# mLSTM stabilisers on all partitions by a transfer through DRAM instead of by matmuls, and three heads in one written order on every engine

## The chip, the cores and the metric

The kernel runs on one core of a Trainium2 chip. The metric is the device time of one execution in microseconds (us). Engines are named as in the profile: PE (TensorE, matmuls) with PEld (its weight loads), DVE (VectorE), ACT (ScalarE), POOL (GpSimd) and SP (SyncE, which here only issues DMAs).

## What is computed

One layer of a hybrid backbone, all in float32: norm and modulation, one input projection, a bidirectional mLSTM (4 heads of width 128) beside a windowed attention, an output projection, and a gated channel mixer. There are 1024 latent tokens and 256 context tokens, width 1024. The change touches the mLSTM, which the reference computes for both directions, first over the context (for its final state) and then over the latent tokens:

```python
def mlstm_scan(q, k, v, log_i, log_f, init, return_h):
    k, v, li, lf = chunk(k), chunk(v), chunk(log_i), chunk(log_f)
    cum = jnp.cumsum(lf, axis=-1)
    cum_end = cum[..., -1]
    g = cum_end[..., None] - cum + li
    m_loc = jnp.max(g, axis=-1)
    w = jnp.exp(g - m_loc[..., None])
    c_loc = jnp.einsum('bhnsd,bhnse->bhnde', w[..., None] * k, v)
    ...
    def step(carry, inp):            # from chunk to chunk
        m_new = jnp.maximum(bt + m_st, m_l)
        a = jnp.exp(bt + m_st - m_new)
        s = jnp.exp(m_l - m_new)
        return (a * c_st + s * c_l, a * n_st + s * n_l, m_new), (c_st, n_st, m_st)
    ...
    a_log = cum + m0[..., None]
    d_log = cum[..., :, None] - cum[..., None, :] + li[..., None, :]
    d_log = jnp.where(order, d_log, -jnp.inf)
    m_t = jnp.maximum(a_log, jnp.max(d_log, axis=-1))        # the stabiliser
    dec = jnp.exp(d_log - m_t[..., None])
    inter = jnp.exp(a_log - m_t)
    s = jnp.einsum('bhntd,bhnsd->bhnts', q, k) * dec
    num = jnp.einsum('bhnts,bhnse->bhnte', s, v) + inter * jnp.einsum('bhntd,bhnde->bhnte', q, c0)
    den = jnp.sum(s, axis=-1) + inter * jnp.einsum('bhntd,bhnd->bhnt', q, n0)
    hid = num / jnp.maximum(jnp.abs(den), jnp.exp(-m_t))
```

The sum of both directions is normalised per head, and multiplied by a gain and the sigmoid of an output gate.

## The kernel before

The kernel works in chunks of 128 tokens: 2 of the context and 8 latent ones (`NC`, `NL`, together `NCH` = 10), and two directions `d`. Projections are made in a split of float32 into a high and a low part (`wh`, `wl`, `hl`), with three matmuls for each product.

**Gates.** `gate_chain` computes for all heads and chunks at once, with one token to a partition, the sums `cum`, the sources `a_` and the stabiliser `M_`, and from them the factors `gi`, `gfl`, `gw`, `gd`. For the decay matrix, the stabiliser is also needed along the free axis: the kernel keeps it in two parts, `mh` and `ml`.

**Heads.** A loop over four heads runs `mlstm(h)`, a generator of 30 steps, and between its steps pieces of another generator that fills PE: `dense(h + 1)`, the projections k, q, v and o of the next head (L537 and the three lines from L298 on), and in the last head `qgen()`, the projection q of the attention. At each step a budget grows by `RATE` us (`RATE3` in the last head; twice at the first step), and pieces are issued until it is used up. A piece names its own length, 0.64 or 1.28 us.

**Steps of `mlstm`.** Two steps with a transpose of a k chunk (`tr`, L601, into the psum tile `pn`; `kwb` and `kwf` are its copies weighted for the two directions), then nine of the backward state: the next transpose, a matmul into `pn` and the update of `cbk` (L631); then the two context chunks of the forward state (`step`, tile `cst`, L651 and L653), then per latent chunk one `first` and one `second`. `first` makes the scores (L664) and the exponent of the decay: three matmuls add, in one psum tile, the causal mask in units of 1e30 (`bigr`, L665) and the stabiliser on all partitions (a matrix of ones times `dm`, which POOL makes as identity times `mh` and `ml`, L660 and L661; L666 and L667). ACT takes the exponential of it into `ee`, DVE multiplies the scores in (L671). `second` multiplies with the states (`pj`, L680 and L681) and with `ee` (`pi`, L683), makes the next forward state, and on ACT and DVE the quotient `hid`.

**Beside that.** The normalisation and gating of a head (`finish`, L712 to L715) is issued in one block within the next head. The output gate's sigmoid is made in place in `ym`, with a tanh on ACT and two instructions on POOL (L641, L642). `ada_second` adds up parts of the adaLN product on DVE from loads of 256 KB (`w`, L731 to L735), eight to a sum, and PE then totals one (`pq`, L740); one whole sum is issued at three of the steps of a head. `load_split` loads weights `wr` and cuts them into `wh` (ACT) and `wl` (DVE, L152).

**Order.** Inside a head `tc.manual_schedule(engines={PE})` keeps the written order on PE alone; on the other engines a scheduler sets it. The psum tiles `pn`, `pe`, `pj`, `pi` and `pq` share a ring of four buffers (`pl`). All DMAs go through the queue of SP.

## Time and profile before

| | |
|---|---|
| time, median of 3 runs | 1331.45 us (1327.45 to 1332.98) |
| the profiled execution | 1331.05 us, its span 1329.1 us |
| busy over the span: PE, DVE, ACT, POOL | 1270.1 (96%), 1000.4 (75%), 610.1 (46%), 329.1 us (25%) |
| granted clock of TensorE, mean | 0.986 |
| the chain that ended last | PE 51%, DVE 8%, ACT 3%, DMA 2% |
| gate chain and projections of head 0 | 97 to 134 us |
| mLSTM of the four heads | 134 to about 400 us, 71 us for head 1 and for head 2 |

Busy time of an engine counts stretches in which it executes; the shares are averages over stages with different limits, so the heads have to be looked at by themselves.

### The profile page before, as it was taken

The numbers are of one execution on the slowest core, as the hardware profiler recorded it, in microseconds if no ns is written. First come the engines' busy times: TensorE is split into PE (matmuls) and PEld (weight loads), VectorE is DVE, ScalarE is ACT, GpSimd is POOL, SyncE is SP. The second block draws the span as 40 slices with busy tenths as digits, with TensorE's granted clock in tenths as the row PEclk, the third lists the DMA queues.
The fourth block names the chain that finished last, engine by engine and source line by source line (L and its number), as shares of the span: only waits on it lengthen the run. The fifth ranks groups of instructions, "written<-read, shape, count | busy, mean of one in ns | idle before, by whom it ended". The sixth has DMA issues, their size and how long they took to land.

```text
span 1329.1 us, 19745 instructions
## 1 busy us (share of the span) xinstructions
PE 1270.1 (96%) x7141; PEld 1082.2 (81%) x7141; DVE 1000.4 (75%) x1819; ACT 610.1 (46%) x1195; POOL 329.1 (25%) x388
## 2 busy tenths in 40 slices
PE   5889999999999899899989999999999999999997
PEld 4689899999989778788867788888888888788886
DVE  5644787866775788988688877777777776876887
ACT  6532244444555576676664333333333333444435
POOL 0440131313346223432330222222122223001000
PEclk9899899999989999999999999999999999999999
DMA  9430444340016422111431333222222325984663
GB/s 357 168 112 33 128 144 143 111 136 5 18 63 192 159 80 96 64 64 49 143 127 48 135 117 105 103 103 99 100 103 103 111 103 193 348 306 151 202 200 137
DMA packets 86017, 171.42 MB, mean 129 GB/s; under 512 B 12672, under 2 KB 25120, under 8 KB 85920
## 3 DMA queue, kind: packets, MB, share of 16 engines
q1 hardware_dynamic: 85632, 169.38, 37.5%
q8 instruction: 56, 0.92, 0.3%
...
q14 instruction: 41, 0.34, 0.1%
HBM read 131.84 MB, written 38.29 MB: 128 GB/s over the span
## 4 chain that ended last, share of the span: by engine, by line
PE 51%; DVE 8%; ACT 3%; DMA 2%; issue 1%; POOL 1%; SPq 0%; ACTq 0%; DVEq 0%; POOLq 0%
PE pd L1808 13%; PE pa L1300 8%; PE pc L1300 8%; PE pe L1300 4%; PE pb L1300 4%; PE pd L1300 4%; PE u L1070 2%; PE po L298 2%; PE po L300 1%; PE po L299 1%; DVE nm L1018 1%; PE pt L1047 1%; DVE hB L1190 1%; DMA ar<-act_s 1%; DVE wl L1190 1%
## 5 line engine op out<-in xcount | busy, mean ns | idle before, releaser
L1402 ACT CAST wh<-Rb 128x1024 fp32r<-128x1024 f32 (+1 forms) x66 | 59.5, 903 | 144.7 <-PE pd L1300 81.6
L1808 PE MATMUL pd<-dh,al 128*128 128x512 f32 x296 | 115.4, 390 | 1.2 <-DVE al L1174 1.2
L1808 PE MATMUL pd<-dh,ah 128*128 128x512 f32 x296 | 115.3, 389 | 0.4 <-ACT ah L1173 0.4
L1808 PE MATMUL pd<-dl,ah 128*128 128x512 f32 x296 | 115.3, 390 | 0.0
L1510 POOL TENSOR_TENSOR tt<-vt,tt 128x512 f32<-128x512 f32 x22 | 29.6, 1344 | 322.7 <-ACT tt L1504 322.7
L1300 PE MATMUL pc<-hB,wh 128*128 128x512 f32 x344 | 106.2, 390 | 1.1 <-DVE av L1379 1.1
L1300 PE MATMUL pa<-hB,wh 128*128 128x512 f32 x336 | 103.5, 389 | 0.0
L1190 DVE TENSOR_TENSOR wl<-Rb,wh 128x1024 fp32r<-128x1024 f32 (+1 forms) x66 | 68.8, 1044 | 39.3 <-ACT wh L1402 38.8
L537 PE MATMUL pp<-hl,wh 128*128 128x512 f32 x256 | 79.8, 403 | 0.0
L1300 PEld LDWEIGHTS pc<-hB,wh 128*128 128x128 f32 x344 | 64.5, 188 | 15.2 <-DVE av L1379 1.6
L298 PE MATMUL pv<-wh,hl 128*128 128x256 f32 x256 | 75.3, 294 | 0.0
L1300 PEld LDWEIGHTS pa<-hB,wh 128*128 128x128 f32 x336 | 63.0, 188 | 13.4 <-ACT sn L1474 0.3
L299 PE MATMUL pv<-wl,hl 128*128 128x256 f32 x256 | 72.8, 284 | 0.0
L300 PE MATMUL pv<-wh,hl 128*128 128x256 f32 x256 | 72.7, 284 | 0.0
L1300 PE MATMUL pc<-hB,wl 128*128 128x512 f32 x172 | 66.9, 389 | 0.0
L1808 PEld LDWEIGHTS pd<-dh,al 128*128 128x128 f32 x296 | 55.6, 188 | 13.4 <-DVE al L1174 1.9
L1808 PEld LDWEIGHTS pd<-dh,ah 128*128 128x128 f32 x296 | 55.6, 188 | 12.3 <-ACT ah L1173 0.8
L1300 PE MATMUL pa<-hB,wl 128*128 128x512 f32 x168 | 65.4, 389 | 0.0
L1808 PEld LDWEIGHTS pd<-dl,ah 128*128 128x128 f32 x296 | 55.6, 188 | 11.7 <-DVE dl L1174 0.3
L660 POOL TENSOR_SCALAR dm<-ident,mh 128x128 fp32r<-128x128 f32 x64 | 28.5, 446 | 131.7 <-PE pe L667 91.1
L298 PE MATMUL px<-wh,hl 128*128 128x256 f32 (+1 forms) x192 | 57.5, 299 | 2.8 <-ACT kr L321 2.8
L300 PE MATMUL px<-wh,hl 128*128 128x256 f32 (+1 forms) x192 | 55.2, 287 | 1.4 <-DVE hl L294 1.4
...
## 6 DMA issues: line engine op xcount, KB each, us to landing
...
br<-in_w_down_dram SPq DMA_DIRECT2D x25, 512.0 KB, 6.0
Ra<-in_w_up_dram SPq DMA_DIRECT2D x22, 512.0 KB, 3.6
Rb<-in_w_up_dram SPq DMA_DIRECT2D x22, 512.0 KB, 3.6
...
wr<-in_w_h_dram SPq DMA_DIRECT2D x16, 512.0 KB, 4.8
```

The lines of the kernel that those rows point to most:

```text
L298: T.matmul(ps, st_hi, mv_hi, start=first, stop=False)
L299: T.matmul(ps, st_hi, mv_lo, start=False, stop=False)
L300: T.matmul(ps, st_lo, mv_hi, start=False, stop=last)
L537: T.matmul(pp[:, 512 * n:512 * n + 512], wkq[sw][:, kt, cs], hl[n][part][:, kt, :], start=kt == 0 and sw + part == 0, stop=kt == KT - 1 an ...
L660: G.tensor_scalar(out=dm[:, d], in0=ident[:], scalar1=mhf[:, d, c, h:h + 1], scalar2=1.0, op0=ALU.mult, op1=ALU.mult)
L1018: V.tensor_reduce(out=self.nm[:, j:j + 1], in_=self.sv[j], axis=AX.X, op=ALU.max, negate=True)
L1070: T.matmul(self.u[:], vv[:, c, self.g], part[i][:, kk * 2 * P:(kk + 1) * 2 * P], start=kb + m == 0, stop=kb == last and m == 1)
L1190: sub = lambda e, o, x, y: e.tensor_tensor(out=o, in0=x, in1=y, op=ALU.subtract)
L1300: T.matmul(ps[:], wt[sw][:, j, ks], hB[part][:, blk, kt, :], start=first and kt == 0 and sw + part == 0, stop=last and kt == 3 and sw == 1 ...
L1402: S.copy(wt[0][:], src)
L1510: G.tensor_tensor(out=self.tt[:, h2_], in0=self.vt[:], in1=self.tt[:, h2_], op=ALU.mult)
L1808: T.matmul(ps[:], ac[sa][:, js], w[sw], start=first and n == 0, stop=last and n == 2, skip_group_check=not fresh)
```

## The change

**Stabiliser.** After the gate chain, two PE transposes turn `M_` into rows, DVE copies them into `rr`, and one DMA writes them to the new DRAM tile `m_d` (40 KB). At the start of each head, one DMA reads that head's 8 x 2 rows of 128 numbers onto all 128 partitions (`ee`, 1 MB, one buffer). DVE adds the mask to it chunk by chunk (`mask`, L619; `tri` is loaded anew with the mask in units of 1e30), ACT takes the exponentials in place (`decay`). The three matmuls, `dm`, `bigr`, `onesr`, `mh` and `ml` go.

**Order.** In heads 0 to 2 the written order now holds for all five engines; in head 3 for PE only, as before. What the scheduler spread before is now spread by hand: convolution and silu of the projections are cut into pieces (`todo`), of which one runs at each piece of the projection; `finish` gives one instruction to a step; `ada_second` gives one piece to a step, loads two ahead, and totals a sum four pieces after its end; raw weights are loaded steps ahead of their cuts.

**Moved.** `kwf`, the scaling of `hid` and the copy of `ym` go from DVE to ACT, the product of the output gate from POOL to DVE (one instruction), `step` from `second` to `first`. RATE goes from 1.4 to 1.5, QB (the latent chunk of v and o before which q is projected) from 2 to 3, TN (the step of the output gate) from 5 to 7.

The core of the diff:

```diff
-RATE = 1.4
+RATE = 1.5
-QB = 2
+QB = 3
-TN = 5
+TN = 7
...
+    m_d = kvp.tile([H * NCH, 2, P], F32, name="m_d")
...
     def gate_chain():
...
-        V.tensor_copy(fl(mh), fl(M_))
-        V.tensor_tensor(out=fl(ml), in0=fl(M_), in1=fl(mh).bitcast(F32), op=ALU.subtract)
...
+        pr = pl.tile([P, 512], F32, name="pr", tag="l")
+        for d in range(2):
+            T.transpose(pr[:40, d * P:d * P + P], M_[:, d].rearrange("p c h -> p (c h)"), ident[:])
+        V.tensor_copy(rr[:], pr[:40, 0:2 * P].rearrange("p (d t) -> p d t", d=2))
+        nc.sync.dma_start(m_d[:], rr[:])
+
+        nc.sync.dma_start(tri[:], I["cst"][:, 3:5])
+        yield
...
+    def conv_silu(dst, ps, w, cb):
+        return [lambda: S.activation(dst, ps[:, :w], AF.Identity, bias=spc("qkc", cb + 3), scale=spc("qkc", cb + 1)),
+                None,
+                lambda: V.scalar_tensor_tensor(out=dst[:, 1:w], in0=ps[:, 0:w - 1], scalar=spc("qkc", cb),
+                                               in1=dst[:, 1:w], op0=ALU.mult, op1=ALU.add),
+                lambda: V.scalar_tensor_tensor(out=dst[:, 0:w - 1], in0=ps[:, 1:w], scalar=spc("qkc", cb + 2),
+                                               in1=dst[:, 0:w - 1], op0=ALU.mult, op1=ALU.add),
+                None,
+                lambda: S.activation(ps[:, :w], dst, AF.Tanh),
+                None,
+                lambda: V.scalar_tensor_tensor(out=dst, in0=ps[:, :w], scalar=1.0, in1=dst, op0=ALU.add, op1=ALU.mult)]
...
+        def work(w):
+            f = todo.pop(0) if todo else None
+            if f:
+                f()
+            return w
...
-                yield 1.28
...
+                yield work(1.28)
+            todo.extend(conv_silu(kT[:, CTX:] if which == 0 else qT[:], pp, SEQ, cb))
...
-            marks.append(V.tensor_copy(ym[:, b, h * DH:(h + 1) * DH], pv[:, DH:2 * DH]).ins)
...
+            S.copy(ym[:, b, h * DH:(h + 1) * DH], pv[:, DH:2 * DH])
...
     def mlstm(h, kT, qT, va):
...
+        ee = tp.tile([P, NL, 2, P], F32, name="ee", tag="ee", bufs=1)
+        nc.sync.dma_start(ee[:], m_d[:].rearrange("(c h) d t -> h c d t", h=H)[h:h + 1, NC:].broadcast_to([P, NL, 2, P]))
...
-                V.tensor_scalar(out=kwf[:, c], in0=pn[:, 0:P], scalar1=g1(gw, 0, c), scalar2=None, op0=ALU.mult)
+                S.activation(kwf[:, c], pn[:, 0:P], AF.Copy, scale=g1(gw, 0, c))
             return pn, kwb
+
+        def mask(b):
+            V.tensor_tensor(out=ee[:, b], in0=ee[:, b], in1=tri[:], op=ALU.add)
+
+        def decay(b):
+            for d in range(2):
+                S.activation(ee[:, b, d], ee[:, b, d], AF.Exp, bias=g1(a_, d, NC + b), scale=-1.0)
...
-            if i == FN and fins:
-                with tc.issue_after(kins[0]):
-                    fins.pop()()
+            if fins and i:
+                next(fins[0])
+            if i:
+                mask(i - 1)
+            if i and i % 2 == 0:
+                decay(i // 2 - 1)
             if i == TN:
...
-                G.tensor_scalar(out=yv, in0=yv, scalar1=1.0, scalar2=1.0, op0=ALU.add, op1=ALU.mult)
-                G.tensor_tensor(out=yv, in0=yv, in1=rwc("gain", h * DH, DH).unsqueeze(1).broadcast_to([P, NL, DH]),
-                                op=ALU.mult)
+                S.activation(yv, yv, AF.Tanh, scale=0.5)
+                V.scalar_tensor_tensor(out=yv, in0=yv, scalar=1.0, in1=rwc("gain", h * DH, DH).unsqueeze(1)
+                                       .broadcast_to([P, NL, DH]), op0=ALU.add, op1=ALU.mult)
...
         def first(c):
...
-            T.matmul(ev, identr[:], bigr[:].rearrange("p d t -> p (d t)"), start=True, stop=False)
-            T.matmul(ev, onesr[:], dm[:, 0:2].rearrange("p d t -> p (d t)"), start=False, stop=False)
-            T.matmul(ev, onesr[:], dm[:, 2:4].rearrange("p d t -> p (d t)"), start=False, stop=True)
...
+            T.matmul(pe[:, 0:P], kT[:, c * P:(c + 1) * P], qT[:, b * P:(b + 1) * P], start=True, stop=True)
+            if b:
+                step(c - 1, pe[:, P:P + E1])
...
+                S.activation(hid[:, b], nm[:, 0, 0:DH], AF.Copy, scale=dn[:, 0:1])
...
     for h in range(H):
+        order_ = {mybir.EngineType.PE}
         if h + 1 < H:
...
+            order_ |= {mybir.EngineType.DVE, mybir.EngineType.Activation, mybir.EngineType.Pool, mybir.EngineType.SP}
...
-        with tc.manual_schedule(engines={mybir.EngineType.PE}):
+        with tc.manual_schedule(engines=order_):
...
-                if n in (0, 9, 18):
-                    with tc.issue_after(marks[-1]) if h == 0 else ExitStack():
-                        ada_next()
...
+                if nh and n in (2, LW):
+                    w = wnext((n // LW,))
...
+                elif nh and n in (24, 27):
+                    wkq = wnext((n // 27,))
...
+                elif nh and n % 8 != 7:
+                    next(ada, 0)
```

On PE, in head 1, one chunk of the forward half with pieces of the next head's projection around it. Before, the scores, the three matmuls of the exponent, six of a projection, and the product with the state:

```order
L664 MATMUL pe<-qT,kT 128x128
L665 MATMUL pe<-bigr,identr 128x256
L666 MATMUL pe<-dm,onesr 128x256
L667 MATMUL pe<-dm,onesr 128x256
L537 MATMUL pp<-hl_171,wh 128x512
L537 MATMUL pp<-hl_542,wh 128x512
L537 MATMUL pp<-hl_171,wl 128x512
L537 MATMUL pp<-hl_542,wl 128x512
L537 MATMUL pp<-hl_172,wh 128x512
L537 MATMUL pp<-hl_543,wh 128x512
L680 MATMUL pj<-cst,qT 128x129
```

And now, from the product with the states of one chunk to the scores of the one after the next:

```order
L687 MATMUL pj<-cst,qT 128x129
L688 MATMUL pj<-cbk,qT 128x129
L690 MATMUL pi<-va,ee 128x129 x2
L548 MATMUL pp<-hl_172,wh 128x512
L548 MATMUL pp<-hl_542,wh 128x512
L548 MATMUL pp<-hl_172,wl 128x512
L548 MATMUL pp<-hl_542,wl 128x512
L548 MATMUL pp<-hl_173,wh 128x512
L548 MATMUL pp<-hl_543,wh 128x512
L676 MATMUL pe<-qT,kT 128x128
L664 MATMUL pe<-va,kwf 128x129
```

The three matmuls are gone, and the projection stands directly behind fp32 matmuls of the chunk at both places; the state's matmul (`pe<-va,kwf`) stands with the scores.

On SP, at the start of head 0, before: the end of the attention's keys and values, weights, and loads `w` of the adaLN sums.

```order
L331 DMA kv_d<-kv 128x256 x3
L147 DMA wr<-in_w_h_dram 128x4x256 x4
L731 DMA w_1491<-in_w_ada_dram 128x512
L731 DMA w_1494<-in_w_ada_dram 128x512
L147 DMA wr<-in_w_h_dram 128x4x256 x2
L731 DMA w_1497<-in_w_ada_dram 128x512
```

And now:

```order
L149 DMA wr<-in_w_h_dram 128x4x256 x2
L501 DMA tri<-in_cst_dram 128x256
L149 DMA wr<-in_w_h_dram 128x4x256 x2
L499 DMA m_d<-rr 40x256
L606 DMA ee<-m_d 128x8x256
L761 DMA w_1494<-in_w_ada_dram 128x512
```

The write of `m_d` and the read of `ee` stand in the queue between the weights and the loads `w` of head 0, whose first one now follows `ee`.

On DVE, in the backward half of head 0, before: updates of `cbk`, the weighted copies `kwf`, adaLN sums, and parts of the convolution of kT.

```order
L735 SCALAR_TENSOR_TENSOR acc<-w_1503,scc,acc 128x512
L631 SCALAR_TENSOR_TENSOR cbk<-cbk,gd,pn 128x129
L735 SCALAR_TENSOR_TENSOR acc<-w_1506,scc,acc 128x512
L607 TENSOR_SCALAR kwf<-pn,gw 128x128
L631 SCALAR_TENSOR_TENSOR cbk<-cbk,gd,pn 128x129
L607 TENSOR_SCALAR kwf<-pn,gw 128x128
L733 TENSOR_SCALAR acc<-w_1678,scc 128x512
L631 SCALAR_TENSOR_TENSOR cbk<-cbk,gd,pn 128x129
L735 SCALAR_TENSOR_TENSOR acc<-w_1681,scc,acc 128x512
L504 SCALAR_TENSOR_TENSOR kT<-pp,sp,kT 128x1023
L607 TENSOR_SCALAR kwf<-pn,gw 128x128
L506 SCALAR_TENSOR_TENSOR kT<-pp,sp,kT 128x1023
```

And now the same part, from the update of the second backward chunk on:

```order
L646 SCALAR_TENSOR_TENSOR cbk<-cst,gd,pn 128x129
L619 TENSOR_TENSOR ee<-ee,tri 128x256
L779 SCALAR_TENSOR_TENSOR acc<-w_1494,scc,acc 128x512
L511 SCALAR_TENSOR_TENSOR kT<-pc__1497,sp,kT 128x255
L646 SCALAR_TENSOR_TENSOR cbk<-cbk,gd,pn 128x129
L619 TENSOR_TENSOR ee<-ee,tri 128x256
L779 SCALAR_TENSOR_TENSOR acc<-w_1535,scc,acc 128x512
L646 SCALAR_TENSOR_TENSOR cbk<-cbk,gd,pn 128x129
L619 TENSOR_TENSOR ee<-ee,tri 128x256
L154 TENSOR_TENSOR wl<-wr,wh 128x1024
L646 SCALAR_TENSOR_TENSOR cbk<-cbk,gd,pn 128x129
L619 TENSOR_TENSOR ee<-ee,tri 128x256
```

A mask (`ee<-ee,tri`) stands behind each `cbk` update, then one piece of an adaLN sum or of another job; `kwf` is gone from DVE. An update of `cbk` now stands behind the mask of the step before it, which needs `ee` from DRAM.

## Rows read from the trace of the kernel before

**Rows 1.** Windows: us, busy (instructions) PE, PEld, DVE, ACT, POOL; PEclk, DMA, GB/s.

```profile
130.00:209.00 79.00, 77.19 (x541) 72.42 (x539) 60.42 (x145) 28.12 (x78) 20.71 (x42) 0.96 0.42 131
209.00:280.00 71.00, 70.98 (x514) 66.13 (x513) 55.48 (x143) 31.07 (x82) 19.16 (x34) 1.00 0.40 123
...
351.00:400.00 49.00, 43.48 (x344) 42.14 (x342) 37.73 (x116) 28.79 (x82) 24.08 (x43) 0.93 0.17 58
```

**Rows 2.** Waits of PE, 97 to 400 us: total us, times, longest.

```profile
PE pj L680 <- DVE cst L653: 2.5, 2, 2.0
PE pq L740 <- DVE cbk L631: 1.8, 1, 1.8
PE pi L683 <- DVE ee L671: 1.5, 1, 1.5
```

**Rows 3.** Timeline of PE, one chunk in head 1: start us, us, instruction.

```profile
244.53 0.36 PE L665 MATMUL pe<-bigr,identr 128*128 128x256 f32 x1
...
244.97 0.63 PE L537 MATMUL pp<-hl,wh 128*128 128x512 f32 x2
245.43 0.61 PE L537 MATMUL pp<-hl,wl 128*128 128x512 f32 x2
...
247.38 0.71 PE L537 MATMUL pp<-hl,wh 128*128 128x512 f32 x2
247.93 0.63 PE L537 MATMUL pp<-hl,wl 128*128 128x512 f32 x2
```

**Rows 4.** Timeline of all engines at the stall in head 0.

```profile
151.82 2.36 POOL L642 TENSOR_TENSOR ym<-ym,rw 128x1024 f32<-128x1024 f32 x1
151.86 2.61 DVE L733 TENSOR_SCALAR acc<-w,scc 128x512 f32<-128x512 f32 x1 [0.69 <-DMA w<-in_w_ada_dram]
...
154.39 0.33 DVE L631 SCALAR_TENSOR_TENSOR cbk<-cbk,gd,pn 128x129 f32<-128x129 f32 x1
```

**Rows 5.** Source line 733: duration ns min/median/max, starts.

```profile
L733 DVE TENSOR_SCALAR acc<-w,scc x8: 476/478/2611, 135.5 to 282.0; 128x512 f32<-128x512 f32 x8
```

**Rows 6.** Windows behind the two stalls (columns as rows 1).

```profile
155.00:161.90 6.90, 6.90 (x34) 6.90 (x34) 6.29 (x11) 1.30 (x2) 0.00 (x0) 0.51 0.44 139
366.60:373.50 6.90, 5.38 (x26) 5.35 (x26) 4.14 (x13) 2.59 (x6) 3.30 (x7) 0.51 0.22 76
```

**Rows 7.** Timeline of all engines at the stall in head 3.

```profile
360.05 2.41 POOL L642 TENSOR_TENSOR ym<-ym,rw 128x1024 f32<-128x1024 f32 x1
...
360.97 4.63 DVE L715 SCALAR_TENSOR_TENSOR ym<-hid,hss,ym 128x128 f32<-128x128 f32 x8
...
365.53 0.34 DVE L653 SCALAR_TENSOR_TENSOR cst<-cst,gd,pn 128x129 f32<-128x129 f32 x1
365.79 1.21 DVE L152 TENSOR_TENSOR wl<-wr,wh 128x1024 fp32r<-128x1024 f32 x1
```

**Rows 8.** Groups of DVE, heads 0 to 2: count, busy us, mean ns.

```profile
L689 DVE TENSOR_TENSOR nm<-pi,nm 128x258 f32<-128x258 f32 x24 | 10.1, 422 | 8.3 <-ACT nm L688 8.3
...
L715 DVE SCALAR_TENSOR_TENSOR ym<-hid,hss,ym 128x128 f32<-128x128 f32 x16 | 4.4, 346 | 0.2
```

**Rows 9.** Timeline at the start of head 0.

```profile
134.43 0.27 PE L601 MATMUL pn<-ident,kT 128*128 128x128 f32 x1
...
142.55 0.35 DVE L631 SCALAR_TENSOR_TENSOR cbk<-cst,gd,pn 128x129 f32<-128x129 f32 x1 [0.50 <-PE pn L621]
```

**Rows 10.** Timeline from head 2 into head 3.

```profile
346.72 0.61 PE L683 MATMUL pi<-va,ee 128*128 128x129 f32 x4
...
354.29 0.27 PE L601 MATMUL pn<-ident,kT 128*128 128x128 f32 x1
```

**Rows 11.** DMA issues, 95 to 440 us: count, KB, median us to landing.

```profile
rga<-row_d SPq DMA_DIRECT2D x1, 512.0 KB, 3.7
row_d<-arw SPq DMA_DIRECT2D x1, 16.0 KB, 1.4
```

**Rows 12.** DMA issues of the whole run.

```profile
wt<-in_w_ada_dram SPq DMA_DIRECT2D x2, 1024.0 KB, 15.6
```

More of the change, by code (lines that the diff above doesn't have):

```diff
@@ L160, in load_split, with rest @@
             load(q)
-        def rest():
+        def rest(qs=range(2)):
             nonlocal hi, lo
-            if not alloc:
+            if hi is None:
                 hi, lo = room()
-            for q in range(2):
+            for q in qs:
                 cut(q)
@@ L578, in dense @@
             if b == QB:
+                while todo:
+                    work(0)
                 yield from kq(1)
@@ L582, in dense @@
             yield 0
+        while todo:
+            work(0)
         if h == 0:
@@ L701, in mlstm @@
             step(c, pn[:, 0:E1])
+            if c == 0:
+                cfs.clear()
+            decay(4 + c)
             yield
-        ee = first(NC)
+        first(NC)
+        tail = None
         yield
         for c in range(NC, NCH):
-            nee = first(c + 1) if c + 1 < NCH else None
+            if c + 1 < NCH:
+                first(c + 1)
+            if tail:
+                next(tail)
             yield
-            second(c, ee)
+            if c < NC + 2:
+                decay(6 + c - NC)
+            if tail:
+                next(tail)
+            tail = second(c)
             yield
-            ee = nee
+        for _ in tail:
+            pass
+        cfs.clear()
         def finish():
@@ L736, in ada_second @@
                                        op1=ALU.add)
+            load(i + 2)
+            if kt == 3 and n:
+                total(n - 1, prev)
+            prev = acc if kt == KT - 1 else prev
+            yield
         yield
-        pq = pl.tile([P, 512], F32, name="pq", tag="l")
-        for j in range(4):
-            T.matmul(pq[:, j:j + 1], acc[:, j * P:(j + 1) * P], ones[:, 0:1], start=True, stop=True)
-        V.tensor_tensor(out=ada2[:, 4 * n:4 * n + 4], in0=pq[:, 0:4], in1=spc("b2", 4 * n, 4), op=ALU.add)
         yield
-    def ada_next():
-        if ada_todo:
-            g = ada_second(ada_todo.pop(0))
-            next(g)
-            if ada_prev:
-                next(ada_prev.pop())
-            ada_prev.append(g)
-        elif ada_prev:
-            next(ada_prev.pop())
+        total(7, prev)
     def row(i):
@@ L850, in qgen @@
                 load_q(0)
-    ada_todo, ada_prev = list(range(8)), []
+    ada = ada_second()
+    ahead_load = lambda h, i: load_split(I["w_h"][h, i] if h < H else I["w_q"][i], 256, split=False, alloc=False)
     wvo = load_split(I["w_h"][0, 1], 256)
+    wnext = ahead_load(1, 0)
     chain = gate_chain()
```

142 lines of the change are left out of this document (66 added, 76 removed).

## The prediction

> **What bounds the kernel now.** I read first the windows over the heads of the mLSTM, the stage that the change touches, then the waits of PE there, then the order of PE around one chunk, then the two places where PE stands still. In head 1 (209 to 280 us) PE is busy for 70.98 of 71 us, with DVE at 55.48, ACT at 31.07 and POOL at 19.16 [rows 1]. So a head costs what PE's instructions cost, and a matmul taken out there shortens the run one for one as long as nothing else becomes late. Head 0 (130 to 209) has 1.8 us without PE and a granted clock of 0.96, and the first 49 us of head 3 have 5.5 us without PE and 0.93 [rows 1]. The waits say for whom: PE waited for DVE in all large cases, 2.5, 1.8 and 1.5 us [rows 2]. Behind each stall stands a second loss: for 6.9 us after it the granted clock is 0.51, the lower of the two levels (1.2 GHz and not 2.4) [rows 6]; at half speed that gives away 6.9 x 0.49 = 3.4 us. A stall of 2 us therefore costs about 5.4.
>
> **The change, part by part.** *The matmuls.* Per latent chunk and head the three matmuls of L665 to L667 go (32 x 3 = 96). On PE the first of them starts at 244.53 and the next projection matmul at 244.97: 0.44 us for the three [rows 3]. Not all of it is saved. A projection pair takes 0.46 (244.97 to 245.43), but the first pair behind a plain fp32 matmul takes 0.55 (247.38 to 247.93) [rows 3], and after the change the projection follows an fp32 matmul directly. So 0.44 - 0.09 = 0.35 per chunk, 32 x 0.35 = **11.2 us** less; the bound above is 32 x 0.44 = 14.1, and no reason makes it less than 11.2, since in heads 1 and 2 PE has no gap in which they could hide. Added are two transposes of M, 0.27 each as the transposes of the heads are [rows 9]: **+0.5**.
>
> *Stall in head 0.* POOL's product of the output gate (L642, 151.82, 2.36 us) and DVE's L733 (151.86, 2.61 us) run together [rows 4]; L733 takes 0.48 otherwise [rows 5]. So DVE is 2.1 us late, the state update L631 behind it comes at 154.39 [rows 4], and PE waits 1.8 us [rows 2], with 3.4 us of clock after it [rows 6]: 1.8 + 3.4 = 5.2. After the change the product stands on DVE (about 1.2 us, as L152 of the same 128x1024 takes 1.21 [rows 7]), and POOL has nothing left in heads 1 and 2: its 34 instructions of head 1 [rows 1] are the 32 `dm` and the two of the gate. The `pq` that stood behind the late L631 now comes four pieces after its sum is done. I take the whole **-5.2**; the bounds are 0 (another late DVE instruction takes its place) and -5.2.
>
> *Stall in head 3.* POOL's L642 at 360.05 again lies beside DVE, whose eight L715 take 4.63 us and hold L653 until 365.53 [rows 7]; eight at the 0.346 of heads 0 to 2 [rows 8] are 2.8. PE waits 2.0 for the state and 1.5 for `ee` [rows 2], and then has the low clock, 3.4 us [rows 6]: 6.9. After the change the normalisation is spread over the pieces, and the product is on DVE. But POOL keeps the rope of the q projection in this head, and `ee` comes late here (below). I take half, **-3.5**, with bounds 0 and -6.9. From L715's start to L642's end (362.46) the two lie beside each other for 1.5 us, against 4.63 - 2.8 = 1.8 us that the eight L715 took too long [rows 7, 8]. The Trainium skill, "SBUF — State Buffer", section "Who interferes with whom", says that such a DVE instruction (two SBUF inputs) and a GpSimd one take a port pair for the whole of an instruction, and the second one blocks. The trace agrees as far as 1.5 goes with 1.8. By that rule the masks, L715 and the gate product, all with two SBUF inputs, would still be held by each rope instruction on POOL, the stall in head 3 would stay, and the sum would be 1315; by the row alone, with L642 gone, it would be 1308.
>
> *DVE and ACT.* From DVE go per head 9 `kwf`, 8 `hid` and 8 `ym` copies, all of 128x128; at the price of L715, of the same tile, 0.346 [rows 8], or a little under it, 25 x 0.34 = 8.5 us. It gets 8 masks of 128x256, at 0.42 as L689 of nearly that size [rows 8], and the gate product of 1.2: 4.6 us. Head 1 then has 55.5 - 3.9 = 51.6 of about 68 us on DVE. ACT gets the 25, at some 0.35 each 9 us: 31 + 9 = 40 of 68. Its 64 exps stay, only their source moves. POOL loses 128 `dm`. All this is off the path while the order written by hand puts nothing ahead of its data; cost **0**, and what it is if not is the second rival.
>
> *The broadcast.* Each head needs 1 MB from DRAM on 128 partitions. No row shows that size in this stretch. The nearest are the broadcast of 512 KB in 3.7 us and the write of 16 KB in 1.4 [rows 11]; through the two, 1 MB takes 3.7 + 512 x 2.3/496 = 6.1 us, an estimate. In head 0 the transposes of M end about 0.5 us after the head's start at 134.43 [rows 9], the copy takes some 0.3 more, the write 1.4: the broadcast is issued at about 136.6 and lands at 142.7. The first mask stands on DVE behind the first L631 of `cbk`, which in the kernel before ran at 142.55 [rows 9]. So it is just in time, and a small lateness falls on DVE alone: the `pn` ring has four buffers and two transposes run ahead, about two steps of 1.5 us or more. In heads 1 and 2 the tile `ee` is free when the last `pi` of the head before has run, at the latest at the next head's start, and the first mask is due 8.1 us after that, as in head 0 (142.55 - 134.43): 8.1 us against 6.1. In head 3 the pieces between the steps are shorter: the third transpose comes at 354.29, and the last `pi` of head 2 ends at 347.33, 7.0 us earlier [rows 10]. The new RATE uses up 30 steps x 0.1 = 3.0 us more of the projection inside the steps, so that 4.0 are left: `ee` is 2 us late there. I cost this at 0 beyond the half already given up: two masks that wait hold `cbk` for 2 us, which the ring covers. The Trainium skill, "DMA: Bandwidth & Descriptors", "Anatomy of one DMA — SWDGE (gpsimd) path", gives 2.0 us and bytes/436e3, which for 1 MB is an estimate of 4.4; by it `ee` would be only 0.4 late in head 3, and the sum would take that stall whole: 1308. No row here has that size in this stretch to tell between them.
>
> *The rest.* The split of conv and silu into pieces, the weights loaded earlier and the adaLN sums in single pieces move work on DVE, ACT and SP, no amount of it. What hides it is the 16 us that DVE has over in a head. The loads `w` go out two pieces ahead of their use, and at the start of each head one of them stands on SP behind the broadcast, which waits for the last `pi`; a late `w` holds `acc`, and DVE behind it.
>
> **Sum.** The profiled execution took 1331.05 us, practically the median of the runs (1331.45). 1331.05 - 11.2 + 0.5 - 5.2 - 3.5 = 1311.7, said as **1312 us**.
>
> **Rivals.** (1) *Only the matmuls are gained.* The two stalls come back at other places, for instance in head 3 with the late `ee`. For it: three of the four heads now have DVE orders in which nothing can pass a waiting instruction. Against it: both old stalls have POOL's L642 beside them [rows 4, 7], and this instruction is gone. Time: 1331.05 - 10.7 = 1320.4.
>
> (2) *DVE or ACT becomes the bound in the written order.* The backward half of a head holds the conv of kT (three passes over 128x1024), two weight cuts of the same size at 1.21 [rows 7], masks, and a sum per piece; one of them in front of a `cbk` update that PE needs gives a stall. One of 2 us in each of heads 0 to 2 costs 3 x (2 + 3.4) = 16.2 us: 1311.7 + 16.2 = 1328, no change that could be measured. For it: a stall of 2.1 us on DVE in head 0 was enough for the loss of before [rows 4]. Against: the share of DVE falls from 55 of 71 to 52 of 68.
>
> (3) *Slower: the broadcast lands late.* 1 MB took 15.6 us at the start of the kernel, among other loads [rows 12]. At that, head 0 has `ee` at 152.2, 9.7 late, less some 3.4 for two steps of ring (1.5 and their own matmuls), plus 3.4 of clock: 9.7. Heads 1 and 2 are 15.6 - 8.1 - 3.4 = 4.1 late, plus 3.4: 7.5 each. Head 3 is 11.6 late, less about 1.2 for its shorter steps, plus 3.4: 13.8. Together 38.5, 1350 us. It decides from a landing of about 12.5 us on (6.6 + 2 x 4.4 + 10.7 = 26.1, 1338 us); below 11.5 heads 1 and 2 do not stall, and heads 0 and 3 alone come to 1327. Against it: loads in this stretch land in 3.7 us for half the size [rows 11]. The Trainium skill speaks against the change here: the same page's "Rules for kernel authors" wants a transfer issued early and its wait late, and here the one buffer of `ee` puts the issue close to the use.
>
> **How the numbers follow.** Forecast (1304 to 1316): 0.48. Only matmuls (1316 to 1324): 0.27. Still better, with a further gain in head 3 or at the ends of the heads: 0.05. DVE or ACT bound (1325 to 1336): 0.13, of which a little ends just under 1324.5. Late broadcast or worse: 0.07. Half a per cent is 6.7 us, about what a measurement of this kernel can tell from no change: faster means below 1324.8, slower above 1338. So faster 0.80, same 0.12, slower 0.08. The range must leave out no more than 2 in 10: it starts at 1303 (all of head 3's stall and a part of 14.1 instead of 11.2) and ends at 1330, inside rival 2. The forecast's own range is 1304 to 1316.
>
> **What would show it.** Heads 1 and 2 should each take 2.8 us less (8 x 0.35), with PE still without gaps; the first `pn` of head 0 to the last of head 2 should hold no granted clock of 0.5. The DMA view should show `ee` landing within 7 us of its issue, the first mask of heads 1 and 2 without a wait, that of head 3 with one of about 2. POOL should be empty in heads 1 and 2. I am wrong if PE's waits name L619, L646 or an exp of `ee` with more than 1 us, if the clock falls in a new place, or if the projection matmuls behind the fp32 ones grow by more than 0.09.

## The result

The changed kernel takes 1319.97 us in the median of 7 runs (1313.41 to 1324.58), the kernel before 1330.73 beside it (7 runs, 1325.58 to 1332.98): a ratio of 0.9921, with a 95% interval of 0.9892 to 0.995. That is 10.8 us less by the medians, where the forecast of 1312 lay 19 below. The profiled execution took 1321.8 us, its span 1319.8.

The stretches between fixed places of PE's timeline show where the time went: the first `pn` transpose of each head, and the last `pi` of head 3 (L601 and L683 before, L609 and L690 after). Times in us, of one profiled execution each, from start to start; the experiments, which follow below, stand in the same table.

| kernel | before head 0 | head 0 | head 1 | head 2 | head 3 | after it | heads together |
|---|---|---|---|---|---|---|---|
| before | 134.4 | 74.9 | 71.1 | 71.2 | 38.9 | 938.6 | 256.1 |
| **after** | 138.0 | 66.9 | 69.0 | 70.2 | 35.2 | 940.6 | 241.2 |
| forecast, against before | +0.5 | -8.0 | -2.8 | -2.8 | -6.3 | 0 | -19.9 |
| measured, against before | +3.6 | -8.0 | -2.1 | -1.0 | -3.7 | +2.0 | -14.9 |
| e1_no_broadcast | 132.4 | 66.9 | 67.7 | 67.9 | 32.4 | 939.2 | 234.9 |
| e2_four_tiles | 135.3 | 66.9 | 67.7 | 67.9 | 30.1 | 939.0 | 232.5 |
| e3_before_gate_on_dve | 132.8 | 72.1 | 72.2 | 71.3 | 39.3 | 938.2 | 254.9 |
| e4_before_no_matmuls | 132.7 | 72.0 | 74.5 | 67.8 | 35.5 | 938.1 | 249.8 |
| e5_sums_moved | 133.3 | 66.9 | 68.1 | 68.1 | 35.2 | 940.6 | 238.3 |
| e6_rate_14 | 135.0 | 69.4 | 69.1 | 68.9 | 34.1 | 936.2 | 241.5 |
| e7_four_tiles_gate_on_pool | 138.1 | 67.2 | 68.3 | 67.9 | 34.0 | 943.8 | 237.3 |
| e8_four_tiles_order_pe_only | 134.1 | 67.3 | 69.5 | 68.9 | 30.6 | 935.3 | 236.3 |
| e9_before_single_sums | 134.0 | 69.7 | 72.0 | 70.3 | 39.3 | 939.2 | 251.2 |
| e10_long_runs | 133.4 | 66.8 | 67.7 | 67.8 | 32.9 | 939.2 | 235.3 |
| e11_four_tiles_long_runs | 133.0 | 66.8 | 67.7 | 67.8 | 30.2 | 938.6 | 232.5 |

The first column goes from 132.4 to 138.1 among variants of the changed kernel that have the same instructions there, or nearly the same, and the column after the heads from 935.3 to 943.8: these are differences between executions, and the 3.6 of the changed kernel's profile is of their size. The +0.5 for the two transposes can't be seen under them. What the change does stands in the heads. The executions of this table are the fastest of their kernel in e1, e3 and e8 and the slowest in e7, and one execution of e9, of 3196 us, is left out of its ratio.

The windows of the heads of the changed kernel, with the columns of [rows 1]:

```profile
138.00:204.80 66.80, 66.80 (x482) 62.36 (x480) 47.00 (x109) 33.80 (x99) 0.00 (x0) 1.00 0.45 129
204.80:273.80 69.00, 68.20 (x490) 63.26 (x489) 51.12 (x126) 37.23 (x105) 0.00 (x0) 1.00 0.44 134
273.80:344.00 70.20, 68.34 (x491) 63.40 (x490) 48.98 (x123) 37.42 (x105) 0.00 (x0) 1.00 0.36 106
344.00:379.20 35.20, 31.43 (x240) 29.75 (x239) 26.23 (x90) 26.90 (x84) 7.15 (x12) 0.90 0.27 84
```

Head 0 has no gap any more, where [rows 1] had 1.8 us and a clock of 0.96, and POOL is empty in the first three heads. But heads 1 and 2 now have gaps of 0.8 and 1.9 us, which they had not, and head 3 still has 3.8 and the low clock. PE's waits from 97 to 440 us say for what (of those of [rows 2], two remain with 0.2 us each and one not at all; they, and those of the q projection and the attention, are left out):

```profile
PE pn L609 <- DVE cst L644: 2.4, 2, 1.7
PE pn L609 <- DVE cbk L646: 2.2, 1, 2.2
PE pn L636 <- ACT kwf L615: 1.4, 3, 1.0
```

All three are `pn`, in the backward halves: the transposes (L609) wait for a buffer of the ring, which DVE frees late, and the state's matmul (L636) waits for ACT. The broadcast, by its source line (us from issue to landing; of its four transfers three show a landing):

```profile
  DVE ee L619: 5.0, 2
...
DMA to landing us min/median/max: 8.2/9.1/9.3
```

9.1 us, not the 6.1 of the estimate. Of DVE's two waits for it, one is in head 0 (1.88 us, which PE does not feel) and one in head 3. The start of head 2, from the timeline of all engines:

```profile
273.48 0.43 SPq L606 DMA_DIRECT2D ee<-m_d  x1
...
275.23 13.08 SPq L761 DMA_DIRECT2D w<-in_w_ada_dram  x4
...
276.66 0.75 DVE L779 SCALAR_TENSOR_TENSOR acc<-w,scc,acc 128x512 f32<-128x512 f32 x1 [1.20 <-DMA w<-in_w_ada_dram]
...
283.99 0.75 DVE L779 SCALAR_TENSOR_TENSOR acc<-w,scc,acc 128x512 f32<-128x512 f32 x1 [6.58 <-DMA w<-in_w_ada_dram]
284.66 0.28 DVE L644 COPY cst<-pn 128x129 f32<-128x129 f32 x1
...
285.00 0.33 PE L609 MATMUL pn<-ident,kT 128*128 128x128 f32 x1 [1.67 <-DVE cst L644]
...
287.14 0.42 DVE L619 TENSOR_TENSOR ee<-ee,tri 128x256 f32<-128x256 f32 x1
```

Behind `ee` (273.48) stand the loads `w` on SP (275.23; the row joins four issues). DVE's next sum piece needs the first of them and waits 6.58 us for it, until 283.99. Everything behind that piece on DVE waits too: the copy of `cst` at 284.66, and with it PE at 285.00, for 1.67 us. The mask at 287.14 has no wait: by then `ee` is there. So in heads 1 and 2 it was not the mask that was held, but a load that had nothing to do with it, in the same queue. In head 3, where the sums are over, it is the mask itself:

```profile
343.44 0.38 SPq L606 DMA_DIRECT2D ee<-m_d  x1
...
348.17 0.35 DVE L646 SCALAR_TENSOR_TENSOR cbk<-cbk,gd,pn 128x129 f32<-128x129 f32 x1
...
351.64 0.76 DVE L619 TENSOR_TENSOR ee<-ee,tri 128x256 f32<-128x256 f32 x2 [3.12 <-DMA ee<-m_d]
351.68 1.28 ACT L623 ACT_TABLE_LOAD   x1 [1.66 <-DMA ee<-m_d]
...
352.32 0.34 DVE L646 SCALAR_TENSOR_TENSOR cbk<-cbk,gd,pn 128x129 f32<-128x129 f32 x1
...
352.72 0.48 PE L609 MATMUL pn<-ident,kT 128*128 128x128 f32 x1 [2.15 <-DVE cbk L646]
...
354.23 0.80 PE L636 MATMUL pn<-va,kwb 128*128 128x129 f32 x2 [1.04 <-ACT kwf L615]
```

`ee`, issued at 343.44, lets the first two masks start at 351.64, after 3.12 us in which DVE stood; the `cbk` update behind them comes at 352.32, and PE has waited 2.15 us for it. ACT stood for `ee` as well, then loaded a table, and gives `kwf` 1.04 us late. A write that DVE and PE don't wait for, issued 1.2 us behind `ee`, lands behind it too (DMA issues, 340 to 352 us):

```profile
row_d<-arw SPq DMA_DIRECT2D x1, 16.0 KB, 7.1
```

It took 1.4 us before the change [rows 11]. What follows is the low clock, in the windows ahead of and behind the stall:

```profile
345.00:352.00 7.00, 5.18 (x41) 4.52 (x39) 2.83 (x7) 5.31 (x15) 0.00 (x0) 1.00 0.56 139
352.30:359.20 6.90, 5.42 (x23) 4.83 (x24) 6.41 (x22) 6.33 (x22) 2.16 (x3) 0.51 0.21 77
```

6.9 us at 0.51 again: 3.4 us, as behind the stalls of before [rows 6]. The stalls in heads 1 and 2 (0.7 and 1.7 us) have no such loss: the clock of these heads is 1.00 in the windows above.

### The profile page after: what moved, and what is told of

Read it like the earlier page. It is cut to its first block, busy times and chain, and to the rows that moved or that the text cites. A ratio compares the mean times of both kernels' runs of the same rounds, so it can differ in the third digit from the quotient of the medians.

```text
span 1319.8 us, 19433 instructions
## 1 busy us (share of the span) xinstructions
PE 1260.1 (95%) x7047; PEld 1070.9 (81%) x7047; DVE 981.3 (74%) x1752; ACT 636.1 (48%) x1295; POOL 258.8 (20%) x252
## 4 chain that ended last, share of the span: by engine, by line
PE 71%; DVE 10%; DMA 4%; ACT 4%; issue 3%; POOL 2%; SPq 0%; ACTq 0%; POOLq 0%; DVEq 0%
PE pd L1857 14%; PE pa L1349 8%; PE pc L1349 8%; PE pp L548 5%; PE pe L1349 4%; PE pd L1349 4%; PE pb L1349 4%; PE u L1119 2%; PE pv L299 2%; PE pv L301 2%; PE pv L300 2%; PE po L299 2%; PE po L301 2%; PE po L300 1%; DVE nm L1067 1%
## 5 line engine op out<-in xcount | busy, mean ns | idle before, releaser
L1239 DVE TENSOR_TENSOR wl<-Rb,wh 128x1024 fp32r<-128x1024 f32 (+1 forms) x66 | 68.9, 1045 | 39.4 <-ACT wh L1451 38.8
L820 POOL TENSOR_TENSOR ta<-z,rope 128x256 f32<-128x256 f32 x16 | 14.3, 895 | 288.7 <-ACT z L816 288.7
L1349 PE MATMUL pc<-hB,wl 128*128 128x512 f32 x172 | 66.9, 389 | 0.0
L299 PE MATMUL px<-wh,hl 128*128 128x256 f32 (+1 forms) x192 | 59.6, 311 | 2.9 <-ACT kr L322 2.9
L301 PE MATMUL px<-wh,hl 128*128 128x256 f32 (+1 forms) x192 | 56.7, 295 | 1.4 <-DVE hl L295 1.4
```

The costliest lines, as they stand in the source:

```text
L299: T.matmul(ps, st_hi, mv_hi, start=first, stop=False)
L301: T.matmul(ps, st_lo, mv_hi, start=False, stop=last)
L820: G.tensor_tensor(out=ta[:].rearrange("p (h e) -> p h e", h=4), in0=q4, in1=rp_(1), op=ALU.mult)
L1239: sub = lambda e, o, x, y: e.tensor_tensor(out=o, in0=x, in1=y, op=ALU.subtract)
L1349: T.matmul(ps[:], wt[sw][:, j, ks], hB[part][:, blk, kt, :], start=first and kt == 0 and sw + part == 0, stop=last and kt == 3 and sw == 1 ...
```

## The experiments

Each ratio is to the kernel before, run beside the experiment; head times are those of the table. The first four take the terms of the sum apart. **The broadcast left out:**

```diff
-        nc.sync.dma_start(ee[:], m_d[:].rearrange(...).broadcast_to([P, NL, 2, P]))
-            V.tensor_tensor(out=ee[:, b], in0=ee[:, b], in1=tri[:], op=ALU.add)
+            V.tensor_tensor(out=ee[:, b], in0=tri[:], in1=tri[:], op=ALU.add)
-                S.activation(ee[:, b, d], ee[:, b, d], AF.Exp, bias=g1(a_, d, NC + b), scale=-1.0)
+                S.activation(ee[:, b, d], ee[:, b, d], AF.Exp, bias=g1(gd, d, NC + b), scale=-1.0)
```

> The changed kernel without the broadcast: the mask is added to itself, so the stabilisers are left out, and the exponentials take another bias of the same shape. All instructions on PE, DVE and ACT stay. If the broadcast and the loads w behind it make the stalls in heads 1 to 3 (0.9 and 1.8 us in heads 1 and 2, some 3.6 of waits and 3.4 of clock at the start of head 3), about 9 to 10 us go: near 1310 us, head 1 and head 2 each near 68.2. If the order written by hand, or ACT, makes them, nothing moves: 1317 to 1323, and PE waits in the same places.

Measured: ratio 0.9864 (0.9831 to 0.9898), median 1314.05. Heads 1 and 2 take 67.7 and 67.9 and PE waits for nothing in heads 0 to 2. The heads together lose 6.3 us against the changed kernel; head 3 has other waits of 1.3 us each, for `nm` from ACT and for the scores in `ee` from DVE, so the sum is under the 9 expected. In heads 1 and 2 the place is the one expected, and the rival falls; in head 3 other waits are left.

**`ee` in four tiles, three of them loaded ahead:**

```diff
+    def load_ee(h, j):
+        eet[h, j] = tp.tile([P, 2, 2, P], F32, name=f"ee{j}", tag=f"ee{j}", bufs=1)
+        nc.sync.dma_start(eet[h, j][:], m_d[:].rearrange("(c h) d t -> h c d t", h=H)[h:h + 1, NC + 2 * j:NC + 2 * j + 2]
+                          .broadcast_to([P, 2, 2, P]))
...
         for c in range(NC, NCH):
+            if h + 1 < H and c - NC in (3, 5, 7):
+                load_ee(h + 1, (c - NC - 3) // 2)
```

> The changed kernel with ee in four tiles of two chunks, each with a transfer of 256 KB; three of the four are issued while the head before still runs, as soon as their chunks are used. If lateness of the broadcast is the cause, the stalls at the starts of heads 1 to 3 go as in the kernel without it, 1310 to 1313 us. If it is the amount of transfer (4 MB beside the loads) and not its place, or the written order, at most 3 us of it go: 1317 to 1323.

Measured: ratio 0.9824 (0.9789 to 0.9858), median 1308.5. With the same 4 MB of transfers and the whole computation, heads 1 and 2 are as without any broadcast, and head 3 takes 30.1 us. The heads together lose 8.7 us against the changed kernel. So it is the one tile and the place of its transfer, not the amount, that cost the change nearly 9 us. In head 3 e2 is 2.3 us below e1, which has no transfer at all, so this part is not lateness of the broadcast; what makes it was not taken apart.

**The kernel before, with the product of the output gate on DVE:**

```diff
-                G.tensor_scalar(out=yv, in0=yv, scalar1=1.0, scalar2=1.0, op0=ALU.add, op1=ALU.mult)
-                G.tensor_tensor(out=yv, in0=yv, in1=rwc("gain", h * DH, DH)...)
+                V.scalar_tensor_tensor(out=yv, in0=yv, scalar=1.0, in1=rwc("gain", h * DH, DH)..., op0=ALU.add, op1=ALU.mult)
```

> The kernel before, with the product of the output gate on DVE as one instruction in place of two on POOL, nothing else. If POOL's product beside DVE makes the two stalls of before, the one in head 0 goes (5.2 us) and at least the half of that in head 3 (3.5): 1320 to 1326 us. If DVE is simply too full there, 1.2 us more on DVE per head make it no better: 1330 or above.

Measured: ratio 1.0007 (0.9983 to 1.0031), the same time. The expectation failed. Head 0 is 2.8 us shorter, but heads 1 and 3 are longer. The timeline of all engines at the old place:

```profile
151.48 0.48 DVE L732 TENSOR_SCALAR acc<-w,scc 128x512 f32<-128x512 f32 x1 [1.18 <-DMA w<-in_w_ada_dram]
...
151.88 1.22 DVE L641 SCALAR_TENSOR_TENSOR ym<-ym,rw 128x1024 f32<-128x1024 f32 x1
...
153.02 0.34 DVE L631 SCALAR_TENSOR_TENSOR cbk<-cbk,gd,pn 128x129 f32<-128x129 f32 x1
...
153.41 1.05 PE L739 MATMUL pq<-ones,acc 128*128 128x1 f32 x8 [1.32 <-DVE cbk L631]
```

L732, which is L733 in [rows 4], is back to 0.48 us, but it has waited 1.18 us for its load, and the product (1.22) now stands behind it on DVE, ahead of the `cbk` update, and PE still waits 1.32 us. POOL's product lengthened L733 by 2.1 us, as read; taking it away is not enough for the stall to go. The windows of heads 0 and 3:

```profile
132.77:204.91 72.14, 70.48 (x506) 65.24 (x505) 57.90 (x141) 27.64 (x75) 14.95 (x32) 1.00 0.47 141
348.39:387.69 39.30, 33.09 (x263) 30.99 (x262) 29.34 (x94) 22.67 (x68) 17.99 (x36) 1.00 0.14 49
```

PE is without work for 1.66 us in head 0, against 1.8 before, and for 6.2 in head 3, and the clock is 1.00 in both. So what head 0 gains in this execution is the low clock and not the stall, and the low clock does not follow every stall. Why it stays away here is not shown.

**The kernel before, without the three matmuls and `dm`** (the exponentials read a constant tile; mask and stabiliser are left out):

```diff
-            T.matmul(ev, identr[:], bigr[:].rearrange("p d t -> p (d t)"), start=True, stop=False)
-            T.matmul(ev, onesr[:], dm[:, 0:2].rearrange("p d t -> p (d t)"), start=False, stop=False)
-            T.matmul(ev, onesr[:], dm[:, 2:4].rearrange("p d t -> p (d t)"), start=False, stop=True)
-                S.activation(ee[:, d], pe[:, d * P:(d + 1) * P], AF.Exp, bias=g1(a_, d, c), scale=-1.0)
+                S.activation(ee[:, d], tri[:, d], AF.Exp, bias=g1(gd, d, c), scale=-1.0)
```

> The kernel before without the three matmuls per chunk, without dm, and without any transfer in their place: the exponentials read a constant tile, so mask and stabiliser are left out. If each three matmuls are worth 0.35 us on PE, heads 1 and 2 take 2.8 us less each, near 68.2, and the run about 11 us: 1319 to 1321, with the stall in head 0 still there. If they are worth the 0.44 that they take, 3.5 a head and 14 in all: 1317. If PE hides them, no change.

Measured: ratio 0.9934 (0.9911 to 0.9957), 8.8 us less in the medians, with the stall in head 0 still there and a new one in head 1 (74.5). Head 2, which has neither, takes 67.8 instead of 71.2. On PE's timeline of one chunk the first pair behind the scores takes 0.55 us (309.05 to 309.60), as the price of the matmuls had it:

```profile
308.91 0.38 PE L660 MATMUL pe<-qT,kT 128*128 128x128 f32 x2
309.05 0.71 PE L537 MATMUL pp<-hl,wh 128*128 128x512 f32 x2
309.60 0.63 PE L537 MATMUL pp<-hl,wl 128*128 128x512 f32 x2
```

The next three ask why the broadcast hurt. **The sum pieces of heads 1 and 2 at other steps:**

```diff
-                elif nh and n % 8 != 7:
+                elif nh and (n % 8 != 7 and not (h and n in (1, 3)) or h and n in (7, 15)):
                     next(ada, 0)
```

> The changed kernel with the adaLN pieces of heads 1 and 2 at other steps: none at steps 1 and 3, whose loads w stand behind the broadcast on SP, two at steps 7 and 15 in their place. The broadcast stays as it is. If DVE is held in heads 1 and 2 by those loads, which come only when the broadcast is through, the backward halves there go from 29.2 and 30.3 us to 27.9 or a little above, and 2 to 3.5 us go in all, with head 3 as it was. If DVE would wait as long for ee itself at the first mask, nothing moves in any head.

Measured: ratio 0.9881 (0.9853 to 0.9908), median 1314.32. Heads 1 and 2 lose 0.9 and 2.1 us, head 3 keeps its 35.2, as expected. DVE's waits for DMA from 97 to 440 us, whose longest for a sum piece was 6.58 above:

```profile
DVE acc L779 <- DMA w<-in_w_ada_dram: 10.3, 15, 1.1
...
DVE ee L619 <- DMA ee<-m_d: 5.7, 2, 3.4
```

So the loads behind the broadcast made the stalls in heads 1 and 2. The Trainium skill, "DMA: Bandwidth & Descriptors", "Queues, rings and completion order", says that each DMA engine starts what a queue gives it in order; the 6.58 us of the changed kernel, its write of 16 KB in 7.1 and this run agree with it.

**RATE alone back at 1.4:**

```diff
-RATE = 1.5
+RATE = 1.4
```

> The changed kernel with RATE at 1.4 as before the change, one number. 3 us more of the projection then lie between the last pi of a head and the start of the next. If the landing of the broadcast sets the stall in head 3, that stall shrinks by 2 to 3 us, those in heads 1 and 2 go, and the run gets 3 to 7 us faster (low clock with it). If the lateness does not matter, no change.

Measured: ratio 0.9891 (0.9864 to 0.9918), median 1315.3, an interval that overlaps the changed kernel's. The 2 to 3 us expected in head 3 did not come: it is 1.1 us shorter and head 2 1.3, but head 0 is 2.5 longer, and the heads together are the same (241.5 and 241.2). It tells little: the number moves other waits too.

**The stabilisers of a head side by side in DRAM**, so that each partition reads one run of 8 KB:

```diff
+            V.tensor_copy(mp[:, d], M_[:, d].rearrange("p c h -> p h c"))
-            T.transpose(pr[:40, d * P:d * P + P], M_[:, d].rearrange("p c h -> p (c h)"), ident[:])
+            T.transpose(pr[:40, d * P:d * P + P], mp[:, d].rearrange("p h c -> p (h c)"), ident[:])
-        nc.sync.dma_start(ee[:], m_d[:].rearrange("(c h) d t -> h c d t", h=H)[h:h + 1, NC:]...)
+        nc.sync.dma_start(ee[:], m_d[:].rearrange("(h c) d t -> h c d t", h=H)[h:h + 1, NC:]...)
```

> The changed kernel with the stabilisers of a head side by side in DRAM, so that a partition of ee reads one run of 8 KB instead of eight of 1 KB; one small DVE copy more in the gate chain. Amount, place and queue of the broadcast stay. If the short runs make it land in 9.1 us instead of the 6.1 that the 512 KB broadcast of runs of 4 KB led to expect, it lands in 5 to 6.5 us, the stall at the start of head 3 shrinks by 2.5 us or more with its low clock, and the run gets 4 to 9 us faster. If the amount or the single source sets it, it still takes 8 to 9 us and nothing moves.

Measured: ratio 0.9873 (0.9842 to 0.9904), median 1309.75. By its DMA issues (count, KB, median us to landing):

```profile
ee<-m_d SPq DMA_DIRECT2D x4, 1024.0 KB, 5.0
```

5.0 us instead of 9.1 for the same 1 MB from the same queue at the same place. Two things differ, though: the runs are longer, and they lie side by side and no longer 4 KB apart; which of the two it is was not taken apart. Heads 1 and 2 are undisturbed, and head 3 is 2.3 us shorter. It keeps another wait, from the timeline of all engines:

```profile
341.71 1.28 ACT L625 ACT_TABLE_LOAD   x1
...
344.26 0.64 PE L638 MATMUL pn<-va,kwb 128*128 128x129 f32 x2 [1.92 <-ACT kwf L617]
```

ACT loads a table and makes two exponentials before the `kwb` and `kwf` that PE needs, and PE waits 1.92 us.

The next three ask what took the stall out of head 0. **Four tiles, with the product back on POOL** (on e2):

```diff
-                V.scalar_tensor_tensor(out=yv, in0=yv, scalar=1.0, in1=rwc("gain", h * DH, DH)..., op0=ALU.add, op1=ALU.mult)
+                G.tensor_scalar(out=yv, in0=yv, scalar1=1.0, scalar2=1.0, op0=ALU.add, op1=ALU.mult)
+                G.tensor_tensor(out=yv, in0=yv, in1=rwc("gain", h * DH, DH)..., op=ALU.mult)
```

> The kernel with four tiles of ee, with the product of the output gate back on POOL in two instructions as before the change. If POOL's product beside DVE is enough for a stall in any order, DVE loses 2 us at that place in each head, and PE shows a wait of 1 us or more in head 0 or head 3: 3 to 12 us slower than with the product on DVE. If the written order has slack there, the same time, within 2 us.

Measured: ratio 0.9848 (0.9819 to 0.9878), against 0.9824 for e2, whose interval overlaps; median 1311.4, 2.9 us above e2's, between the two expectations. Heads 0 to 2 hardly notice (at most 0.6 us), head 3 is 3.9 us longer. At its start, from the timeline of all engines:

```profile
344.23 3.29 DVE L627 TENSOR_TENSOR ee<-ee,tri 128x256 f32<-128x256 f32 x2 [1.16 <-DMA ee<-m_d]
...
344.85 2.38 POOL L667 TENSOR_TENSOR ym<-ym,rw 128x1024 f32<-128x1024 f32 x1
...
347.44 0.28 DVE L652 COPY cst<-pn 128x129 f32<-128x129 f32 x1
...
347.78 0.33 PE L617 MATMUL pn<-ident,kT 128*128 128x128 f32 x1 [2.80 <-DVE cst L652]
```

Two masks, 0.76 us in the changed kernel, take 3.29 beside POOL's product of 2.38, and PE waits 2.80 us behind them. The Trainium skill, "SBUF — State Buffer", "Who interferes with whom", says that an instruction of DVE with two SBUF inputs contends with one of POOL that reads SBUF, for a port pair that is an exclusive lock: 0.76 + 2.38 = 3.14 agrees with 3.29. In heads 0 to 2 the product finds slack.

**Four tiles, with the written order on PE alone** (on e2):

```diff
-            order_ |= {mybir.EngineType.DVE, mybir.EngineType.Activation, mybir.EngineType.Pool, mybir.EngineType.SP}
+            pass
```

> The kernel with four tiles of ee, where the written order of heads 0 to 2 holds for PE alone and the scheduler sets DVE, ACT, POOL and SP, as in the kernel before. If it is the written order on all engines that took the stall out of head 0, it comes back there, with the lower clock: 2 to 6 us slower, head 0 at 69 or more. If it is the spreading of the sums, the conversions and the normalisation over the steps, the time stays within 2 us of the kernel with the written order.

Measured: ratio 0.9879 (0.9835 to 0.9924), median 1314.76 (1307.75 to 1320.39); its interval overlaps that of e2, whose median is 6 us lower. Head 0 is 67.3, so the stall does not come back without the written order. Heads 1 and 2 are 1.8 and 1.0 us longer, so the order on all engines is worth some 3 us there, in the one execution that has a profile; what makes up the rest of the 6 us is open.

**The kernel before, with single sum pieces** (`ada_second` as in the changed kernel, in place of the one with a whole sum):

```diff
-    ada_todo, ada_prev = list(range(8)), []
+    ada = ada_second()
...
-                if n in (0, 9, 18):
-                    with tc.issue_after(marks[-1]) if h == 0 else ExitStack():
-                        ada_next()
+                if nh and n % 8 != 7:
+                    next(ada, 0)
```

> The kernel before, with the adaLN sums made as in the changed kernel, one piece to a step with its load two ahead, and nothing else: POOL's product, the matmuls and the scheduler's order stay. If the blocks of eight pieces on DVE are what makes the state update late in head 0 and lets PE wait at pq, head 0 loses the 5.2 us (74.9 to about 70), heads 1 and 2 stay: 1325 to 1328 us. If POOL's product beside DVE is enough, the stall stays and the time with it: 1331.

Measured: ratio 0.9981 (0.9961 to 1.0001), on the edge of no change; the heads together lose 4.9 us in the profiled execution. Head 0 is 69.7, 5.2 us less: the stall and its low clock are gone, with POOL's product still there. The timeline of all engines where L733 stood:

```profile
151.35 2.40 POOL L642 TENSOR_TENSOR ym<-ym,rw 128x1024 f32<-128x1024 f32 x1
...
151.62 1.28 DVE L504 SCALAR_TENSOR_TENSOR kT<-pp,sp,kT 128x1023 f32<-128x1023 f32 x1 [0.56 <-ACT kT L503]
```

Beside the product there is now a pass of the convolution, which reads PSUM and takes 1.28 us, no more than in e3, where POOL is empty. In the windows from there on PE has no gap, and the clock stays up:

```profile
150.00:157.00 7.00, 7.00 (x60) 6.90 (x59) 5.37 (x9) 2.99 (x5) 3.45 (x2) 1.00 0.00 0
157.00:164.00 7.00, 7.00 (x56) 6.69 (x55) 4.20 (x10) 1.22 (x5) 1.42 (x4) 1.00 0.27 78
```

The sums in blocks, with a total on PE behind each, were what the stall needed; POOL's product made it longer. Pieces and totals moved together here, so they are not told apart.

The last one puts the two cures of the broadcast together. **Four tiles and long runs** (e2 with the lines of e10; the transfer of a tile reads):

```diff
-        nc.sync.dma_start(eet[h, j][:], m_d[:].rearrange("(c h) d t -> h c d t", h=H)[h:h + 1, NC + 2 * j:NC + 2 * j + 2]...)
+        nc.sync.dma_start(eet[h, j][:], m_d[:].rearrange("(h c) d t -> h c d t", h=H)[h:h + 1, NC + 2 * j:NC + 2 * j + 2]...)
```

> Both together, four tiles of ee issued ahead and the long runs. In the kernel with four tiles the transfers are already out of the way, so it should be the same as that one within 2 us, about 1308; if transfers still hold DVE or the loads w there, 2 to 4 us less.

Measured: ratio 0.9833 (0.9816 to 0.985), median 1306.3 us (1305.45 to 1306.87): as e2, which was expected, and faster than both kernels.

## Why the prediction came out as it did

**The matmuls were right.** 0.35 us a chunk was forecast. From one `pj` to the next, over the same fill, PE takes 4.46 us before (312.95 to 317.41) and 4.11 in e4 (310.52 to 314.63), as in the changed kernel. The timelines of PE, before and in e4:

```profile
312.95 0.39 PE L680 MATMUL pj<-cst,qT 128*128 128x129 f32 x2
317.41 0.39 PE L680 MATMUL pj<-cst,qT 128*128 128x129 f32 x2
```

```profile
310.52 0.38 PE L673 MATMUL pj<-cst,qT 128*128 128x129 f32 x2
314.63 0.38 PE L673 MATMUL pj<-cst,qT 128*128 128x129 f32 x2
```

The heads without a stall go from 71.1 to 67.7, 3.4 and not 2.8. The other half microsecond lies at one place of heads 1 and 2 before, which the prediction read as free of gaps; in head 1, from the timeline of all engines:

```profile
226.52 1.05 POOL L641 TENSOR_SCALAR ym<-ym 128x1024 f32<-128x1024 f32 x1 [25.56 <-ACT ym L640]
226.53 1.57 DVE L735 SCALAR_TENSOR_TENSOR acc<-w,scc,acc 128x512 f32<-128x512 f32 x1 [0.27 <-DMA w<-in_w_ada_dram]
228.03 0.34 DVE L631 SCALAR_TENSOR_TENSOR cbk<-cbk,gd,pn 128x129 f32<-128x129 f32 x1
228.42 0.33 PE L601 MATMUL pn<-ident,kT 128*128 128x128 f32 x1
```

A sum piece takes 1.57 us beside the first gate instruction on POOL, where the one at that place in head 2 of e4 takes 0.75, and the `cbk` update and PE's next instructions come some 0.45 us late. Head 2 of before has the same. It is the stall of head 0 in small, and it is gone in head 2 of e4 and in e1; that POOL makes it was not tried alone.

**Head 0 was right in size, -8.0, and half right in its reason.** POOL's product and L733 do hold each other, but e3 and e9 show that the product alone did not make the stall, nor its move take it away: in the kernel before it goes when the sums are spread (5.2 us), and when only the product moves, 2.8 us of it go in head 0, by the clock alone, and 1.6 come back in the other heads. The change did both. The price of 3.4 us of clock behind every stall was too general: it came in head 3 of the changed kernel, but not in its heads 1 and 2 and not in e3.

**The broadcast was wrong, and this is the step that failed: it cost 8.7 of the 23.6 us that the heads could give (e2).** The prediction put the landing at 6.1 us, costed it at 0 "beyond the half already given up", and called a wait of two masks one "which the ring covers". It landed in 9.1 us. The row it was drawn through, the broadcast of 512 KB in 3.7 us [rows 11], reads runs of 4 KB, while `ee` reads runs of 1 KB; e10 shows that the layout, runs of 8 KB side by side, makes 4.1 us of difference. In head 0 the ring covered a wait of 1.88 us, as the prediction had it; in head 3, where DVE waited 3.12, it did not, and PE stood 2.15 us and then had the low clock. And the load `w` in the queue behind the broadcast was named in "The rest" ("a late `w` holds `acc`, and DVE behind it") but given no price: in heads 1 and 2 it cost 0.9 + 2.1 us by e5. Together the one tile and its place cost 8.7 us in the heads by e2, and 6.3 by e1. With it mended (e2) they take 23.6 us less than before, 3.7 more than the 19.9 forecast: 2.5 of that is head 3, where most of the old stall goes once `ee` is in time and not half, and 0.5 to 0.6 is from each of heads 1 and 2. The rope on POOL, by which the prediction's 1315 kept that stall, made none in e2: PE has no single wait above 0.6 us in its heads. Of the prediction's own signs of being wrong two came: a wait for L646 of 2.2 us, and a low clock at a new place, in head 3.

**The rivals.** 1319.97 lies above the forecast's own range (1304 to 1316) and at the first rival, "only the matmuls are gained" (1320). That rival's account holds in part: the stall of head 3 comes back with the late `ee` that it names, and smaller ones come in heads 1 and 2, but the stall of head 0 is gone, and the broadcast took 8.7 of the 12.1 us that the two old stalls were worth. That the time meets 1320 so closely is partly chance. The third rival had the mechanism, with 12.5 us as the point from which the run would be slower, and 11.5 as the point below which heads 1 and 2 would not stall. They did at 9.1, through `w`. Of the second, that DVE or ACT becomes the bound, the changed kernel shows no more than a wait of 1 us; e10, where `ee` is in time, shows that ACT, which got `kwf` by the change, holds PE for 1.92 us in head 3. QB, TN and the moves to ACT were not tried alone.
